# A depthwise convolution of 31 taps moved from four engines to TensorE, as products of four taps by 32 channels

## The chip, the cores and the metric

The kernel runs on one core of a Trainium2 chip. The metric is the device time of one execution in microseconds. The kernel before took 1886.85 us, the median of three runs (1884.89 to 1888.67).

## What is computed

Two layers of a decoder trunk for one sequence of 512 tokens with 1024 channels, in float32. Layer 0 is a state-space mixer beside a dilated attention, layer 1 a causal convolution module; each layer ends with a gated FFN. Only the convolution module of layer 1 is touched:

```python
def causal_depthwise_conv(x, w, b):
    k = w.shape[0]                       # 31 taps
    out = lax.conv_general_dilated(
        x, w[:, None, :].astype(x.dtype), window_strides=(1,), padding=[(k - 1, 0)],
        dimension_numbers=('NWC', 'WIO', 'NWC'), feature_group_count=x.shape[-1])
    return out + b
```

It stands between a pointwise product with a gate (a, g = x W1 + b1; u = a * sigmoid(g)) and a layer norm over the channels, a silu, and a second pointwise product.

## The kernel before

Channels lie on partitions, in eight channel tiles k of 128; tokens are the columns, in two halves H0 (columns 0 to 255) and H1 (256 to 511). Weights come in slabs of 256 output channels: SP issues the load (L185), ScalarE casts them to a high part in fp32r (L193), VectorE or GpSimd subtracts to get the low part (L194). A product of one channel tile is 24 matmuls (L206, L207, L209: high by high, low by high, high by low). The buffers of a slab (loaded, high, low) are there twice.

The module runs as follows. `first_banks` makes the products of channel tiles 0 and 1 (tiles p_a in the rows) while the norm before it is still being finished. The loop over j and i then makes two products for each other channel tile, pa and pg; ScalarE takes the sigmoid of pg (cth, L965), VectorE multiplies (u, tag cu). The convolution of a channel tile and a half goes to one of three places, by hand-written tables (WORK, GATE, HOLD, ORDER):

- five pieces to GpSimd: for each tap ScalarE multiplies (pr, L989) and GpSimd adds (cv, L990);
- seven pieces to VectorE, one multiply-add in PSUM for each tap (cps, L997);
- channel tile 6 (dgx, L1012) and channel tile 7 (dg, L1015 to L1017) to TensorE, as products with diagonal matrices, one for each tap: tile 6 in fp32, tile 7 as three fp32r products of high and low parts. The diagonals are built by GpSimd (`diagonals`, L909): those of tile 6 at 876 us, those of tile 7 while the module's first products run.

Then `layer_norm` of a half (means mu, L1028; variances var; the spread lnr_b; silu L1047 and cast L1048 on ScalarE) and `pw2` (products pq). GpSimd adds the second bias to the residual (xT, L1073). Instructions of one engine run in the order that a scheduler fixed when the program was built; the order of the program is where it starts from, and `tc.issue_after` holds an instruction behind another one.

Of the kernel before, what the change touches and what calls it, by code (L numbers as in the profile page):

```python
# [17 lines left out]
P = 128  # L18
T = 512
# [24 lines left out]
C_ID, C_TRI, C_W = 0, P, 2 * P  # L44


def shape_constants():
# [4 lines left out]
    c[:, C_TRI:C_TRI + P] = i[:, None] <= i[None, :]  # L52

# [23 lines left out]
def trunk_kernel(ctx: ExitStack, tc, a, out, dbg=None):  # L77
# [15 lines left out]
    cst = const.tile([P, C_W], F32, name="cst")  # L93
    nc.sync.dma_start(cst, a["k_cst"])
# [171 lines left out]
    def spread(v, nb, name):  # L266

        dg = tmp.tile([P, nb, P], F32, tag="diag", name=name + "_d", bufs=1)
        for b in range(nb):
            marks["spread"] = V.tensor_scalar(dg[:, b, :], ident, v[:, b:b + 1], None, op0=ALU.mult)  # L270
        ps = bank("C", name + "_b", (P, nb * P))
        for b in range(nb):
            marks['lnr'] = PE.matmul(ps[:, b * P:(b + 1) * P], ones, dg[:, b, :], start=True, stop=True)
        return ps
# [622 lines left out]
    dwh = const.tile([P, 248], F32R, name="dwh")  # L897
    dwl = const.tile([P, 248], F32, name="dwl")
    S.copy(dwh, taps)
    V.tensor_tensor(dwl, taps, dwh.bitcast(F32), op=ALU.subtract)  # L900

    def tapw(t, k):
        return taps[:, t * KT + k:t * KT + k + 1]
# [8 lines left out]
    X = 6  # L912
    ctx_d = ExitStack()
    pre = ctx_d.enter_context(tc.tile_pool(name="pre", bufs=1))
    dgx = pre.tile([P, TAPS, P], F32, name="dgx")
    diagonals(dgx, taps, X)
# [22 lines left out]
    R = [k for k in range(7) if k != X]  # L939
    WORK = {G: ((R[0], H0), (R[2], H0), (R[0], H1), (R[2], H1), (R[5], H1)),  # L940
            V: ((R[1], H0), (R[3], H0), (R[4], H0), (R[5], H0), (R[1], H1), (R[3], H1), (R[4], H1))}
    PRT = (2, 2)
    WQG = [(0, 2), (0, 3)] + [(H1.start, j) for j in range(4)]
    GATE = {(X, H1.start): ((14, 'var'), (24, 'lnr')), (7, H1.start): ((0, 'lnr'),)}
    HOLD, held = {(R[3], H1.start): 24, (R[4], H1.start): 8}, []
    ORDER = (R[0], R[1], R[3], R[2], R[4], X, R[5], 7)
    with tc.tile_pool(name="conf", bufs=2) as conf:
        dg = [conf.tile([P, TAPS, P], F32R, tag=f"dg{i}", name=f"dg{i}", bufs=1) for i in range(2)]
        for d, w in zip(dg, (dwh.bitcast(F32), dwl)):
            diagonals(d, w, 7)  # L950
        h = nxt.finish(const, g_mix1, mod[1][:, 0:8], XG)
        w1 = a["cv_w_pw1"][0]
        us, parts = [], {}
        for j in range(4):
            ws = [slab([(w1[:, o + j * 256:o + (j + 1) * 256], KT, 256)], f"wp{o}_{j}") for o in (0, D)]
            banks = first_banks(ws, h, "p", nxt.cuts) if j == 0 else None
            for i in range(2):
# [8 lines left out]
                u = conf.tile([P, PAD + T], F32, tag="cu", name=f"cu{k}", bufs=KT)  # L966
                V.memset(u[:, 0:PAD], 0.0)
                V.scalar_tensor_tensor(u[:, PAD:], pa_, b1[:, k:k + 1], th, op0=ALU.add, op1=ALU.mult)
                us.append(u)
                if k == 7:  # L970
                    uh = conf.tile([P, PAD + T], F32R, tag="cuh", name=f"cuh{k}", bufs=1)
                    ul = conf.tile([P, PAD + T], F32R, tag="cul", name=f"cul{k}", bufs=1)
                    S.copy(uh, u)
                    V.tensor_tensor(ul, u, uh.bitcast(F32), op=ALU.subtract)
                    parts[k] = uh, ul
        cv = {}

        def conv(k, c, eng):
            n, w = f"{k}_{c.start}", c.stop - c.start
            o = cv[k, c.start] = conf.tile([P, w], F32, tag="cv" + n, name="cv" + n, bufs=1)  # L980

            def tap(src, t):
                return src[:, c.start + t:c.stop + t]

            if eng is G:
                S.activation(o, tap(us[k], 0), AF.Identity, bias=bdw[:, k:k + 1], scale=tapw(0, k))
                for t in range(1, TAPS):
                    pr = conf.tile([P, w], F32, tag=f"pr{WORK[G].index((k, c)) % PRT[0]}", name=f"pr{n}_{t}", bufs=PRT[1])
                    S.mul(pr, tap(us[k], t), tapw(t, k))  # L989
                    G.tensor_tensor(o, o, pr, op=ALU.add)  # L990
            elif eng is V:
                ps = bank("B", f"cps{n}", (P, w))
                V.tensor_scalar(ps, tap(us[k], 0), tapw(0, k), bdw[:, k:k + 1], op0=ALU.mult, op1=ALU.add)

                def run(lo, hi):
                    for t in range(lo, hi):
                        V.scalar_tensor_tensor(o if t == TAPS - 1 else ps, tap(us[k], t), tapw(t, k), ps,  # L997
                                               op0=ALU.mult, op1=ALU.add)

                cut = HOLD.get((k, c.start), TAPS)  # L1000
                run(1, cut)
                if cut < TAPS:
                    held.append(lambda: run(cut, TAPS))
# [19 lines left out]
        def layer_norm(c):  # L1023
# [3 lines left out]
            for i, k in enumerate(ORDER):  # L1027
                PE.matmul(mb, meanw, cv[k, n], start=i == 0, stop=i == KT - 1)  # L1028
# [104 lines left out]
```

## Time and profile before

| | |
|---|---|
| time, median of three runs | 1886.85 us (1884.89 to 1888.67) |
| the profiled execution | 1896.6 us, span 1894.8 us |
| granted clock of TensorE, mean | 0.968 |
| busy: PE, DVE, ACT, POOL | 1770.6, 1150.2, 761.5, 564.4 us |
| convolution module, first products to the last of pw_2 | 1258.6 to 1508.4 us |

PE is the matmul unit, PEld its weight loads, DVE is VectorE, ACT ScalarE, POOL GpSimd, SP the engine that issues DMAs. Times of rows count from the start of the span. An fp32 matmul has two records on PE, an fp32r matmul one. The duration of a record is longer than the distance to the next, since matmuls are pipelined; what a product costs is the distance between starts. Line numbers are those of the kernel before; in the changed kernel, shared lines before L894 have numbers higher by one.

### The profile page before, as it was taken

How to read it: one execution, taken by the hardware profiler on the slowest of the kernel's cores; microseconds unless marked ns; L12 is line 12 of the kernel's file. 1: busy time of each engine (PE TensorE's matmuls, PEld its weight loads, DVE VectorE, ACT ScalarE, POOL GpSimd, SP SyncE). 2: the span in 40 equal slices, each digit the busy share in tenths (PEclk: the TensorE clock that was granted, in tenths of full speed). 3: DMA queues.
4: the chain of work that ended last, by engine and by line, in shares of the span. 5: the costliest groups of instructions: out<-in, count | busy, mean ns of one | idle time of the engine just before them, and what ended most of it. 6: DMA issues, size and time to landing. Idle time of an engine off the chain costs nothing.

```text
span 1894.8 us, 24381 instructions
## 1 busy us (share of the span) xinstructions
PE 1770.6 (93%) x9277; PEld 1475.4 (78%) x9277; DVE 1150.2 (61%) x2168; ACT 761.5 (40%) x1476; POOL 564.4 (30%) x486
## 2 busy tenths in 40 slices
PE   5897979999999999989999999979899899999998
PEld 3675767777788778768888888878799888888887
DVE  7859687755655565458774673386896643333336
ACT  6333333335445454245222222346775432122225
POOL 1437786412443340003000000056993400000001
PEclk8998989999999999999999999989999899999999
DMA  8354545634544543434655553242211423322223
GB/s 302 99 138 141 149 129 138 158 99 140 141 122 139 135 133 105 130 102 134 222 182 173 186 192 93 92 149 62 73 45 35 132 79 105 97 89 95 83 94 129
DMA packets 225779, 238.94 MB, mean 126 GB/s; under 512 B 11755, under 2 KB 195885, under 8 KB 225662
## 3 DMA queue, kind: packets, MB, share of 16 engines
q1 hardware_dynamic: 214525, 195.44, 34.4%
q0 software_dynamic: 11136, 41.95, 6.7%
q8 instruction: 73, 1.20, 0.3%
q14 instruction: 45, 0.36, 0.1%
HBM read 228.72 MB, written 8.64 MB: 125 GB/s over the span
## 4 chain that ended last, share of the span: by engine, by line
PE 73%; DVE 11%; DMA 6%; ACT 4%; issue 3%; POOL 2%; SPq 0%; DVEq 0%; POOLq 0%; ACTq 0%
PE fd L206 4%; PE fd L209 4%; PE fd L207 4%; PE fg L207 4%; PE fg L206 4%; PE fu L206 4%; PE fu L207 4%; PE fu L209 4%; PE fg L209 4%; PE cps L1012 2%; DMA ar<-a_dram 1%; PE s L716 1%; PE z L206 1%; PE z L207 1%; PE qq L206 1%
## 5 line engine op out<-in xcount | busy, mean ns | idle before, releaser
L248 POOL TENSOR_TENSOR n_acc<-n_acc,n_q 128x256 f32<-128x256 f32 x32 | 27.6, 864 | 545.6 <-ACT n_q L244 545.5
L194 DVE TENSOR_TENSOR wf_l<-wf_w,wf_h 128x1024 fp32r<-128x1024 f32 x88 | 106.1, 1241 | 75.7 <-ACT wf_h L193 75.7
L206 PE MATMUL fd<-uh,wd_h 128*128 128x512 f32 (+1 forms) x448 | 150.0, 351 | 0.9 <-DVE xT L591 0.9
L207 PE MATMUL fd<-uh,wd_l 128*128 128x512 f32 (+1 forms) x448 | 147.8, 346 | 0.0
L193 ACT CAST wf_h<-wf_w 128x1024 fp32r<-128x1024 f32 x88 | 87.6, 1047 | 117.5 <-PE fd L209 73.4
L207 PE MATMUL fg<-n_h,wf_l 128*128 128x512 f32 x320 | 126.0, 394 | 2.0 <-DVE wf_l L194 2.0
L206 PE MATMUL fg<-n_h,wf_h 128*128 128x512 f32 x320 | 126.2, 394 | 0.7 <-ACT wf_h L193 0.5
L206 PE MATMUL fu<-n_h,wf_h 128*128 128x512 f32 x320 | 124.8, 390 | 0.0
L207 PE MATMUL fu<-n_h,wf_l 128*128 128x512 f32 x320 | 124.7, 390 | 0.0
L990 POOL TENSOR_TENSOR cv<-cv,pr 128x256 f32<-128x256 f32 x150 | 113.7, 792 | 16.9 <-ACT pr L989 14.7
L171 POOL TENSOR_TENSOR adap<-adap 128x128 f32<-128x128 f32 (+2 forms) x96 | 104.6, 1094 | 4.7
L868 DVE TENSOR_TENSOR fs<-fs,fu 128x512 f32<-128x512 f32 x40 | 27.5, 688 | 129.1 <-PE fu L209 129.1
L591 DVE SCALAR_TENSOR_TENSOR xT<-fd,mod,xT 128x512 f32<-128x512 f32 (+1 forms) x64 | 39.1, 615 | 101.6 <-PE fd L209 101.3
L742 ACT ACTIVATE s<-s,nm 128x128 f32<-128x128 f32 x192 | 79.4, 416 | 47.4 <-DVE nm L738 38.4
L193 ACT CAST wd_h<-wd_w 128x1024 fp32r<-128x1024 f32 (+1 forms) x64 | 57.1, 940 | 103.0 <-PE fd L209 82.8
L169 POOL TENSOR_TENSOR adap<-adap,cs 128x1024 f32<-128x1024 f32 x32 | 68.2, 2131 | 88.9 <-DMA adap<-in_ada_w 88.9
L206 PEld LDWEIGHTS fd<-uh,wd_h 128*128 128x128 f32 x448 | 84.3, 188 | 13.1 <-DVE xT L591 1.3
L209 PE MATMUL fd<-ul,wd_h 128*128 128x512 f32 (+1 forms) x448 | 93.2, 346 | 0.0
L207 PEld LDWEIGHTS fd<-uh,wd_l 128*128 128x128 f32 x448 | 84.3, 188 | 11.0
L194 DVE TENSOR_TENSOR wd_l<-wd_w,wd_h 128x1024 fp32r<-128x1024 f32 (+1 forms) x64 | 67.7, 1090 | 34.9 <-ACT wd_h L193 34.8
L997 DVE SCALAR_TENSOR_TENSOR cps<-cu,taps,cps 128x256 f32<-128x256 f32 x203 | 86.9, 481 | 1.5
L161 DVE SCALAR_TENSOR_TENSOR adaa<-adaw,cs,adaa 128x512 f32<-128x512 f32 x112 | 84.8, 758 | 2.6
(418 smaller groups left out, 4913.6 us busy)
## 6 DMA issues: line engine op xcount, KB each, us to landing
adaw<-in_ada_w POOLq DMA_DIRECT2D x24, 1024.0 KB, 5.6
wf_w<-in_ffn_w_gate SPq DMA_DIRECT2D x22, 1024.0 KB
wf_w<-in_ffn_w_up SPq DMA_DIRECT2D x22, 1024.0 KB, 5.4
adap<-in_ada_w POOLq DMA_DIRECT2D x32, 512.0 KB, 5.5
wd_w<-in_ffn_w_down SPq DMA_DIRECT2D x16, 1024.0 KB, 5.2
wd_w<-in_ffn_w_down SPq DMA_DIRECT2D x16, 768.0 KB, 4.4
wa_w<-in_hy_w_out SPq DMA_DIRECT2D x20, 512.0 KB, 4.1
adaw<-in_ada_w SPq DMA_DIRECT2D x8, 1024.0 KB, 7.6
```

The lines of the kernel that those rows point to most:

```text
L161: V.scalar_tensor_tensor(acc, ws[k // 4][:, k % 4, :], cs[:, k:k + 1], acc, op0=ALU.mult, op1=ALU.add)
L169: G.tensor_tensor(w3, w3, cs.unsqueeze(2).broadcast_to([P, KT, P]), op=ALU.mult)
L171: G.tensor_tensor(w[:, 0:n], w[:, 0:n], w[:, n:2 * n], op=ALU.add)
L193: S.copy(hi[:, s:e], raw[:, s:e])
L194: eng.tensor_tensor(lo[:, s:e], raw[:, s:e], hi[:, s:e].bitcast(F32), op=ALU.subtract)
L206: PE.matmul(ps[:, cols], hi[:, o(k):o(k) + P], xh, start=k == 0, stop=False)
L207: PE.matmul(ps[:, cols], lo[:, o(k):o(k) + P], xh, start=False, stop=False)
L209: PE.matmul(ps[:, cols], hi[:, o(k):o(k) + P], acts[k][1][:, cols], start=False, stop=k == nk - 1)
L591: V.scalar_tensor_tensor(xT[m][:, cols], ps[:, cols], mod[l][:, go + m:go + m + 1], xT[m][:, cols], op0=ALU.mult, op1=ALU.add)
L742: S.activation(s[:, o:o + wd], s[:, o:o + wd], AF.Exp, bias=nm, accum_out=l)
L990: G.tensor_tensor(o, o, pr, op=ALU.add)
L997: V.scalar_tensor_tensor(o if t == TAPS - 1 else ps, tap(us[k], t), tapw(t, k), ps, op0=ALU.mult, op1=ALU.add)
```

## The change

All taps go to TensorE, with another form of product. For a channel tile, the 128 partitions of the moving operand hold four shifts of 32 channels: u4[k][32 s + c, g, t] is u of channel 32 g + c at column t + s. Its stationary partner, 128 by 32, holds on the partitions of shift s a diagonal of the 32 channels with tap 4 m + s. So one product adds four taps for 32 channels, and writes to the 32 partitions of group g; eight values of m by four groups make 32 fp32 products for a channel tile. The built program places them on strips of the array of 128 rows by 32 columns, at column 0, 32, 64 and 96 in turn. Channel tiles 0 to 3 run on 512 columns (128 products), 4 to 7 on each half (256 products).

The shifted copies are made by 16 DMAs on SP for each channel tile (`shifted`), the stationary operands by one GpSimd instruction (`filters`) from the columns wcol, which 16 small VectorE copies make once. ScalarE evicts and adds the bias. The tables WORK, GATE, HOLD, ORDER and the `issue_after` are gone; u has three buffers in place of eight. The slabs of pw_2 are split on GpSimd for the first half and on VectorE for the second.

```diff
-    def diagonals(d, w, k):
-        for t in range(0, TAPS, 8):
-            e = min(TAPS, t + 8)
-            w3 = w.rearrange("p (t k) -> p t k", k=KT)[:, t:e, k:k + 1]
-            G.tensor_tensor(d[:, t:e, :], ident.unsqueeze(1).broadcast_to([P, e - t, P]),
-                            w3.broadcast_to([P, e - t, P]), op=ALU.mult)
...
+    wcol = const.tile([P, KT, 4, 8], F32, name="wcol")
+    V.memset(wcol[96:128, :, :, 7], 0.0)
+    taps3 = taps.rearrange("p (t k) -> p k t", k=KT)
+    for sft in range(4):
+        for g in range(4):
+            o = wcol[sft * 32:(sft + 1) * 32, :, g, 0:8 if sft < 3 else 7]
+            V.tensor_copy(o, taps3[g * 32:(g + 1) * 32, :, sft:TAPS:4])
+    id4 = const.tile([P, 32], F32, name="id4")
+    nc.sync.dma_start(id4, a["k_cst"][:, C_I4:C_W])
...
+    def filters(k):
+        w4[k] = pre.tile([P, 32, 32], F32, tag="w4", name=f"w4_{k}", bufs=4)
+        G.tensor_tensor(w4[k], id4.unsqueeze(1).broadcast_to([P, 32, 32]),
+                        wcol[:, k, :, :].rearrange("p g m -> p (g m)").unsqueeze(2).broadcast_to([P, 32, 32]), op=ALU.mult)
+
+    for k in range(4):
+        filters(k)
...
+        def shifted(k, u):
+
+            u4[k] = conf.tile([P, 4, T + 28], F32, tag="u4", name=f"u4_{k}", bufs=5)
+            for sft in range(4):
+                for g in range(4):
+                    nc.sync.dma_start(u4[k][sft * 32:(sft + 1) * 32, g, :], u[g * 32:(g + 1) * 32, sft:sft + T + 28])
+
+        def conv(k, cols):
+            n, w = f"{k}_{cols[0].start}", cols[-1].stop - cols[0].start
+            ps = bank("A" if k % 2 else "B", f"cps{n}", (P, w))
+            for m in range(8):
+                for g in range(4):
+                    t = cols[0].start + 4 * m
+                    PE.matmul(ps[g * 32:(g + 1) * 32, :], w4[k][:, g * 8 + m, :], u4[k][:, g, t:t + w],
+                              start=m == 0, stop=m == 7)
+            for c in cols:
+                o = cv[k, c.start] = conf.tile([P, T // 2], F32, tag=f"cv{k}_{c.start}", name=f"cv{k}_{c.start}", bufs=1)
+                S.activation(o, ps[:, c.start - cols[0].start:c.stop - cols[0].start], AF.Identity, bias=bdw[:, k:k + 1])
...
-                u = conf.tile([P, PAD + T], F32, tag="cu", name=f"cu{k}", bufs=KT)
+                u = conf.tile([P, PAD + T + 1], F32, tag="cu", name=f"cu{k}", bufs=3)
...
+                shifted(k, u)
+                if k >= 2:
+                    conv(k - 2, CUTS if k < 6 else CUTS[:1])
+                    if k < 6:
+                        filters(k + 2)
...
-        for e, work in WORK.items():
-            for k, c in work:
-                conv(k, c, e)
-        conv(X, H0, PE)
-        conv(7, H0, PE)
-        layer_norm(CUTS[0])
-        with tc.issue_after(marks["spread"].ins):
-            for run in held:
-                run()
-        conv(X, H1, PE)
-        conv(7, H1, PE)
+        for k in (6, 7):
+            conv(k, CUTS[:1])
+        layer_norm(H0)
+        for k in (4, 5, 6, 7):
+            conv(k, CUTS[1:])
```

In the built program this moves instructions at three places. In the names, w is a filter or a slab, u the shifted copies, cps the PSUM tile of a convolution.

On TensorE, between the projections of channel tiles 5 and 6, the kernel before goes straight from one to the next:

```order
L209 MATMUL pg_0_10481<-n_l_9903,wp_2_h 128x512
L209 MATMUL pg_0_10481<-n_l_9904,wp_2_h 128x512
L206 MATMUL pa_0_10527<-n_h_9889,wp_3_h 128x512
L207 MATMUL pa_0_10527<-n_h_9889,wp_3_l 128x512
L206 MATMUL pa_0_10527<-n_h_9890,wp_3_h 128x512
```

and the changed kernel has the convolution of channel tile 3 there:

```order
L210 MATMUL pg_0_10697<-n_l_9912,wp_2_h 128x512
L210 MATMUL pg_0_10697<-n_l_9913,wp_2_h 128x512
L959 MATMUL cps_0_10745<-u_3_10488,w_3_7057 32x512 x32
L207 MATMUL pa_0_10800<-n_h_9898,wp_3_h 128x512
L208 MATMUL pa_0_10800<-n_h_9898,wp_3_l 128x512
```

A convolution now stands behind each product pg from tile 2 on, two channel tiles behind the projection; before, all products of the convolution stood behind the last pg.

At the end of the layer norm of the first half, the changed kernel has this on TensorE ahead of pw_2 (pq):

```order
L1005 MATMUL var_11113<-ones,cvq_0_11142 128x1 x4
L959 MATMUL cps_256_11308<-u_7_10964,w_7_10782 32x256 x32
L995 MATMUL mu_11351<-cv_256_10428,meanw 128x256
L995 MATMUL mu_11351<-cv_256_10540,meanw 128x256
L995 MATMUL mu_11351<-cv_256_10668,meanw 128x256
L995 MATMUL mu_11351<-cv_256_10780,meanw 128x256
L995 MATMUL mu_11351<-cv_256_11236,meanw 128x256
L274 MATMUL lnr_b<-lnr_d,ones 128x128 x2
...
L207 MATMUL pq_0_0_0_11458<-ch_11016,wq_0_h 128x256
L208 MATMUL pq_0_0_0_11458<-ch_11016,wq_0_l 128x256
```

Of the second half's convolution, only the rest of tile 5 and tile 7 stand behind the first half's statistics; before, all products of tiles 6 and 7 of the second half stood there, but for fourteen taps of tile 6.

In SP's queue the kernel before has the slabs of the module one behind the other:

```order
L185 DMA wp_0_w<-in_cv_w_pw 128x8x256 x2
L185 DMA wp_1_w<-in_cv_w_pw 128x8x256 x2
L185 DMA wp_2_w<-in_cv_w_pw 128x8x256 x2
L185 DMA wp_3_w<-in_cv_w_pw 128x8x256 x2
L185 DMA wq_0_w<-in_cv_w_pw 128x8x256
```

and the changed kernel

```order
L186 DMA wp_1_w<-in_cv_w_pw 128x8x256 x2
L951 DMA u_0_10264<-cu_10260 32x540 x16
L951 DMA u_1_10287<-cu_10283 32x540 x16
L951 DMA u_2_10376<-cu_10372 32x540 x16
L186 DMA wp_2_w<-in_cv_w_pw 128x8x256 x2
L951 DMA u_3_10488<-cu_10484 32x540 x16
L186 DMA wp_3_w<-in_cv_w_pw 128x8x256 x2
L951 DMA u_4_10616<-cu_10612 32x540 x16
L186 DMA wq_0_w<-in_cv_w_pw 128x8x256
```

The copies of tiles 0 to 2 are issued ahead of the slabs of tiles 4 and 5 (wp_2), and each later slab has sixteen copies ahead of it.

On GpSimd, the eight instructions that build the diagonals dg, ahead of the additions to xT, are gone; before:

```order
L909 TENSOR_TENSOR dg_9879<-cst,dwh 128x1024 x3
L909 TENSOR_TENSOR dg_9879<-cst,dwh 128x896
L909 TENSOR_TENSOR dg_9880<-cst,dwl 128x1024 x3
L909 TENSOR_TENSOR dg_9880<-cst,dwl 128x896
L1073 TENSOR_SCALAR xT_216<-xT_216,gb_9872 128x512
```

and now, where the additions are followed by the filters of tiles 4 to 7:

```order
L1033 TENSOR_SCALAR xT_223<-xT_223,gb_9891 128x512
L914 TENSOR_TENSOR w_4_10430<-id_7046,wcol 128x1024
L914 TENSOR_TENSOR w_5_10542<-id_7046,wcol 128x1024
L914 TENSOR_TENSOR w_6_10670<-id_7046,wcol 128x1024
L914 TENSOR_TENSOR w_7_10782<-id_7046,wcol 128x1024
L195 TENSOR_TENSOR wq_0_l<-wq_0_w,wq_0_h 128x1024 x2
```

## Rows read from the trace of the kernel before

**Rows 1.** The profile page: its first part (busy time, share of the span and instructions of each engine), the share by engine of the chain that ended last, and three rows of the costliest groups (line, engine, operation, tile, count, then busy time and mean ns of one, then the idle time before them).

```profile
PE 1770.6 (93%) x9277; PEld 1475.4 (78%) x9277; DVE 1150.2 (61%) x2168; ACT 761.5 (40%) x1476; POOL 564.4 (30%) x486
...
PE 73%; DVE 11%; DMA 6%; ACT 4%; issue 3%; POOL 2%; SPq 0%; DVEq 0%; POOLq 0%; ACTq 0%
...
L193 ACT CAST wf_h<-wf_w 128x1024 fp32r<-128x1024 f32 x88 | 87.6, 1047 | 117.5 <-PE fd L209 73.4
...
L990 POOL TENSOR_TENSOR cv<-cv,pr 128x256 f32<-128x256 f32 x150 | 113.7, 792 | 16.9 <-ACT pr L989 14.7
...
L997 DVE SCALAR_TENSOR_TENSOR cps<-cu,taps,cps 128x256 f32<-128x256 f32 x203 | 86.9, 481 | 1.5
```

**Rows 2.** The windows, one row for each stretch, in order of time: the first products of the FFN of layer 0; the first four products of the convolution module; its other twelve; convolution and layer norm; the products of pw_2; the first products of the FFN of layer 1. Columns: start and end, length in us, then busy time (and instructions) of PE, PEld, DVE, ACT and POOL, the clock granted to TensorE, the busy share of the DMA engines and their GB/s.

```profile
879.20:908.20 29.00, 27.16 (x202) 26.72 (x202) 25.32 (x54) 14.76 (x32) 9.36 (x7) 0.89 0.43 145
1258.60:1299.00 40.40, 30.40 (x204) 29.20 (x204) 29.01 (x55) 16.01 (x32) 30.45 (x16) 0.83 0.18 53
1299.00:1377.70 78.70, 70.30 (x289) 55.90 (x289) 68.26 (x128) 59.61 (x114) 67.17 (x87) 0.96 0.26 81
1377.70:1439.20 61.50, 61.50 (x371) 56.86 (x370) 59.94 (x148) 44.73 (x94) 46.57 (x64) 0.94 0.11 35
1439.20:1508.40 69.20, 61.82 (x443) 60.89 (x443) 39.13 (x84) 31.37 (x61) 34.64 (x20) 0.85 0.30 94
1508.50:1535.20 26.70, 25.27 (x207) 24.48 (x205) 16.88 (x48) 14.74 (x32) 0.00 (x0) 1.00 0.23 74
```

**Rows 3.** The timeline of the module's first products, rows of VectorE, GpSimd and PE: start and duration in us, engine, line, operation, tiles, count, and in brackets the idle time before and what ended it.

```profile
1255.36 2.35 DVE L194 TENSOR_TENSOR wp_l<-wp_w,wp_h 128x1024 fp32r<-128x1024 f32 x2
1258.36 8.12 DVE L308 SCALAR_TENSOR_TENSOR n_l<-n_g,mod,n_h 128x256 fp32r<-128x256 f32 x4
1267.10 5.08 DVE L194 TENSOR_TENSOR wp_l<-wp_w,wp_h 128x1024 fp32r<-128x1024 f32 x2
1287.63 1.67 DVE L308 SCALAR_TENSOR_TENSOR n_l<-n_g,mod,n_h 128x256 fp32r<-128x256 f32 x4
...
1258.34 7.85 POOL L909 TENSOR_TENSOR dg<-cst,dwh 128x1024 fp32r<-128x1024 f32 x4 [3.46 <-PE fd L209]
1266.16 9.63 POOL L909 TENSOR_TENSOR dg<-cst,dwl 128x1024 fp32r<-128x1024 f32 x4
1276.80 6.36 POOL L1073 TENSOR_SCALAR xT<-xT,gb 128x512 f32<-128x512 f32 x4 [1.01 <-ACT n_g L305]
...
1266.92 0.58 PE L206 MATMUL p_a<-n_h,wp_h 128*128 128x256 f32 x1 [6.38 <-DVE xT L591]
```

**Rows 4.** The waits of PE from 1296 to 1378 us: waiting instruction and releaser, then idle us in all, number of waits, the longest.

```profile
PE pa L206 <- ACT cth L965: 7.6, 5, 1.9
PE pa L207 <- DVE wp_l L194: 0.8, 1, 0.8
```

**Rows 5.** PE's timeline around the longest of these waits.

```profile
1330.44 0.39 PE L206 MATMUL pg<-n_h,wp_h 128*128 128x512 f32 x1
...
1334.07 1.97 PE L209 MATMUL pg<-n_l,wp_h 128*128 128x512 f32 x8
1337.97 0.50 PE L206 MATMUL pa<-n_h,wp_h 128*128 128x512 f32 x1 [1.93 <-ACT cth L965]
...
1340.40 0.63 PE L206 MATMUL pa<-n_h,wp_h 128*128 128x512 f32 x1
1340.82 0.63 PE L207 MATMUL pa<-n_h,wp_l 128*128 128x512 f32 x1
```

**Rows 6.** PE's timeline of the first half's convolution: the products of channel tile 6, and the first means, which follow those of channel tile 7.

```profile
1377.93 13.55 PE L1012 MATMUL cps<-cu,dgx 128*128 128x256 f32 x62
...
1402.41 3.62 PE L1028 MATMUL mu<-cv,meanw 128*128 128x256 f32 x16
```

**Rows 7.** One of the three lines of channel tile 7, both halves: shortest, median and longest ns of a record, then the start of the first and of the last.

```profile
L1015 PE MATMUL cps<-cuh,dg x62: 276/281/469, 1391.1 to 1437.3; 128*128 128x256 f32 x62
```

**Rows 8.** PE's timeline in layer 0: eight products with 64 stationary columns, which stand alternately in the left and the right half of the array, and four with 128 stationary columns, all in fp32 with 128 moving columns.

```profile
116.59 1.09 PE L503 MATMUL pd<-ar,xdt 128*64 128x128 f32 x16
...
128.04 1.16 PE L515 MATMUL po<-sc,prev 128*128 128x128 f32 x8
```

**Rows 9.** Weight loads of 32 and of 64 columns, by line and shape: busy time, mean ns of one, idle time before.

```profile
L431 PEld LDWEIGHTS acs_t<-cst,acs 128*32 128x32 f32 x4 | 0.4, 96 | 0.2
...
L503 PEld LDWEIGHTS pd<-ar,xdt 128*64 128x64 f32 x256 | 14.0, 136 | 6.3 <-issue 5.3 <-DVE ar L499 0.6 <-DVE sx L445 0.3
```

**Rows 10.** ScalarE's timeline in the second half's layer norm: silus (L1047, two in each of the rows) and casts.

```profile
1464.68 0.39 ACT L1048 CAST ch<-cv 128x256 fp32r<-128x256 f32 x1
1464.98 1.09 ACT L1047 ACTIVATE cv<-cv,pb 128x256 f32<-128x256 f32 x2
1465.98 0.39 ACT L1048 CAST ch<-cv 128x256 fp32r<-128x256 f32 x1
1466.27 1.09 ACT L1047 ACTIVATE cv<-cv,pb 128x256 f32<-128x256 f32 x2
```

**Rows 11.** The timeline of SP's queue: issues of small transfers.

```profile
839.07 1.23 SPq L787 DMA_DIRECT2D at<-w_dram  x2
841.60 0.36 SPq L106 DMA_DIRECT2D dw_r<-in_cv_w_dw  x1
```

**Rows 12.** DMA issues: tiles, queue, count, KB each, median us from issue to landing.

```profile
dw_r<-in_cv_w_dw SPq DMA_DIRECT2D x1, 64.0 KB, 2.2
wp_w<-in_cv_w_pw SPq DMA_DIRECT2D x8, 1024.0 KB, 5.6
```

More of the change, by code (lines that the diff above doesn't have):

```diff
@@ L938, in trunk_kernel @@
     H0, H1 = CUTS
[L939 to L946, printed above, removed]
     with tc.tile_pool(name="conf", bufs=2) as conf:
-        dg = [conf.tile([P, TAPS, P], F32R, tag=f"dg{i}", name=f"dg{i}", bufs=1) for i in range(2)]
-        for d, w in zip(dg, (dwh.bitcast(F32), dwl)):
-            diagonals(d, w, 7)
         h = nxt.finish(const, g_mix1, mod[1][:, 0:8], XG)
         w1 = a["cv_w_pw1"][0]
-        us, parts = [], {}
+        cv, u4 = {}, {}
+        def shifted(k, u):
[14 more added lines that the diff above has]
+                S.activation(o, ps[:, c.start - cols[0].start:c.stop - cols[0].start], AF.Identity, bias=bdw[:, k:k + 1])
         for j in range(4):
@@ L976, in trunk_kernel @@
[L976 to L1003, printed above, removed]
-            else:
-                ps = bank("A", f"cps{n}", (P, w))
-                gates = {t: marks[m] for t, m in GATE.get((k, c.start), ()) if m in marks}
-                gate = None
-                for t in range(TAPS):
-                    gate = gates.get(t, gate)
-                    with tc.issue_after(gate.ins) if gate else nullcontext():
-                        if k == X:
-                            PE.matmul(ps, dgx[:, t, :], tap(us[k], t), start=t == 0, stop=t == TAPS - 1)
-                            continue
-                        (uh, ul), (dh, dl) = parts[k], (d[:, t, :] for d in dg)
-                        PE.matmul(ps, dh, tap(uh, t), start=t == 0, stop=False)
-                        PE.matmul(ps, dh, tap(ul, t), start=False, stop=False)
-                        PE.matmul(ps, dl, tap(uh, t), start=False, stop=t == TAPS - 1)
-                S.activation(o, ps, AF.Identity, bias=bdw[:, k:k + 1])
@@ L1026, in layer_norm @@
             mb = bank("A", f"mu{n}", (P, w))
-            for i, k in enumerate(ORDER):
+            for i, k in enumerate(range(KT)):
                 PE.matmul(mb, meanw, cv[k, n], start=i == 0, stop=i == KT - 1)
             vp = bank("C", f"var{n}", (P, nb))
-            for i, k in enumerate(ORDER):
+            for i, k in enumerate(range(KT)):
                 t = cv[k, n]
@@ L1033, in layer_norm @@
                 if i % 2 == 0:
-                    spare = {0: us[R[0]], 6: us[R[2]]}
-                    two = spare[i] if i in spare else tmp.tile([P, T], F32, tag="st_sq", name=f"cvq{k}_{n}")
+                    two = tmp.tile([P, T], F32, tag="st_sq", name=f"cvq{k}_{n}")
                 sq = two[:, i % 2 * w:(i % 2 + 1) * w]
@@ L1038, in layer_norm @@
                 for b in range(nb):
-                    marks['var'] = PE.matmul(vp[:, b:b + 1], sq[:, b * P:(b + 1) * P], ones[:, 0:1], start=i == 0 and b == 0,
+                    PE.matmul(vp[:, b:b + 1], sq[:, b * P:(b + 1) * P], ones[:, 0:1], start=i == 0 and b == 0,
                               stop=i == KT - 1 and b == nb - 1)
```

35 lines of the change are left out of this document (11 added, 24 removed).

## Prediction

> **What bounds the kernel now.** The page comes first. TensorE is busy for 93% of the span and holds 73% of the chain that ended last; the taps on GpSimd (113.7 us) and VectorE (86.9 us) are large, but stand beside it [rows 1]. Taking them away is therefore worth only what they make TensorE wait for. So the second view is the windows of the stretch that the change touches [rows 2]. The first four products of the convolution module take 40.4 us, of which PE works 30.4; the same stage in the two FFNs takes 29.0 and 26.7. The other twelve products take 78.7 us with PE busy for 70.3. Then PE is busy without a gap for 61.5 us with convolution and layer norm.
>
> The timeline tells why the first stage is long [rows 3]. GpSimd builds the diagonals of channel tile 7 from 1258.3 to 1275.8 us, and in just that time VectorE's instructions are slow: n_l takes 2.03 us (8.12 for four) against 0.83 later (1.67 for two), a slab's subtraction 2.54 (5.08 for two) against 1.18 before. PE waits 6.4 us there for VectorE. While GpSimd then adds gb to xT, PE has no such wait. The waits of the twelve products are 7.6 us for ScalarE's sigmoid, which stands among the tap multiplications in ScalarE's order, and 0.8 for a slab [rows 4]. After such a wait the granted clock falls as well: behind the one at 1337.97 us the products start 0.43 us apart for a while, where they had 0.227 (sixteen from 1330.44 to 1334.07) [rows 5]; that is the 1.2 GHz level, and the engine had stood still for 1.9 us before it.
>
> **What goes.** On TensorE: channel tile 6 takes from 1377.93 to the first record of tile 7 at 1391.1, 13.2 us for 31 fp32 products of 256 columns, or 0.425 each; tile 7 takes to 1402.41, 11.3 us [rows 6, 7]. Two halves: 2 x 24.5 = **49.0 us less**. The waits of the twelve products: the sigmoid has no tap ahead of it any more, **8.4 less**. Their clock: twelve products are 288 x 0.227 = 65.4 us, they were busy for 70.3 [rows 2, 5]; of the 4.9 I let 1.3 stay, **3.6 less**. The first stage: without diagonals it should be as long as in the FFNs, 26.7 to 29.0, so 11.4 to 13.7 less; nothing would be less if another wait took over. I take the end that two stages show: **12 less**. GpSimd now adds gb to xT there earlier (6.36 us for four), which slowed nobody [rows 3], and so cost nothing; without that cover it would come back as part of the 12. The diagonals of tile 6 give way to four filters in the same place of GpSimd's order, next to work that PE does not wait for: nothing. The sixteen copies of taps on VectorE before that: nothing to 1 us, I take nothing.
>
> **What comes.** On TensorE 128 products of 512 columns and 256 of 256, with 32 stationary columns each, in groups of four that write to four different strips of 32 partitions. The time depends on how many run at once. One at a time: 256 x 0.425 + 128 x 0.850 = 217.6 us; two at a time 108.8; four at a time 54.4. The nearest rows are products with 64 stationary columns that alternate between two halves of the array: eight of them (16 records) take 1.09 us, no more than four full-width ones (8 records, 1.16 us) [rows 8]. So two ran at once with no loss. Four is the same pattern with narrower strips; I take **54.4 more**, and keep 108.8 as the far end. Where PE goes from one width to the other, its pipe has to run empty: a record lasts 0.28 us and the next starts 0.12 behind it (93 products in 11.3 us) [rows 6, 7], so 0.16 on a side, 0.3 for each of about ten blocks: **3 more** (0 to 5).
>
> The evictions (12 on ScalarE) and the four filters of the later tiles on GpSimd stand beside the products; the bank is used again only two blocks later. They cost nothing as long as ScalarE, now without 150 tap multiplications, is on time.
>
> The start of pw_2: before, the layer norm of the first half was covered by the 24.5 us of the second half's products. Now behind its statistics stand only the rest of tile 5, tile 7 and the means of the second half, some 8 us. ScalarE needs for each channel tile a silu (0.55) and a cast (0.39, starting 0.3 apart when they follow each other) and a square of the other half, near 1.1 us, 8.8 for eight [rows 10]. pw_2's first products take them channel by channel. I take **5 more**, between 0 (all covered) and 8.8 (nothing covered).
>
> The shifted copies: 128 transfers in SP's queue, sixteen per channel tile, each 69 KB. A transfer of this size took 0.36 us to issue and 2.2 to land; two others took 0.62 each [rows 11, 12]. The slab loads stand behind them: wp_2 behind u_0 to u_2, 48 x 0.36 = 17.3 us. With it due about 35 us after the first stage (four projections 21.8, two convolutions 13.6), and needing 5.6 to land, 2.1 for the casts [rows 1, 12] and 1.3 for a subtraction, it has 26 us for the 48 issues, or 0.54 each. At 0.36 nothing waits: **0**. At 0.62 wp_2 is some 5 us late and u_7 some 3: **8** is the upper bound from these rows. u_5 to u_7 also stand behind slab loads that wait for a buffer; those buffers come free about when the product ahead of the copy ends.
>
> **The sum.** -49.0 + 54.4 + 3 - 8.4 - 3.6 - 12 + 5 = **-10.6 us**. It is made in the profiled execution, whose time is 1896.6 us (span 1894.8), 9.75 above the median of 1886.85; I carry the difference over to the median: **1876 us**. What a measurement can tell from no change is about 0.2%, 3.8 us, so this is faster, though by no wide margin.
>
> **Rivals.**
> (A) Slower: the weight loads set the pace. An fp32 product has two records and so two loads, 768 loads in all. With four products at once a load must start every 54.4 / 768 = 71 ns on average. A load of 32 columns takes 96 ns, one of 64 columns 136 [rows 9]. If they go one after another, the convolution takes 768 x 0.096 = 73.7 us, 19.3 over my term: **1895**. It decides from 65 us on (54.4 + 10.6), when a load costs more than 85 ns, or fewer than 3.35 products run at once. For it: nothing in this trace has four strips. Against it: in the rows with two strips 16 loads of 136 ns fit into 1.09 us, one per 68 ns [rows 8, 9], so loads do overlap. I give it 0.17.
> The Trainium skill ("TensorE: Matmul & The Clock Gate", Measured speedup vs the span model) gives 2.38 times for three column tiles and 3.07 for four row tiles, less than the number of tiles. At 3.07 the convolution would be 217.6 / 3.07 = 70.9 us and the time 1893, an estimate from that page; the trace's two strips show no such loss. The skill also says ("TensorEngine Tiling (Array Packing)", Key Properties) that column tiling goes without the fast weight load, which would work for this rival; no run here shows its price for 32 columns.
> (B) Only two at once, as the trace shows it and no more: 54.4 over my term, **1930**. The four strips are given in rotation, and two halves that are halved again need nothing new, so 0.07.
> (C) The copies are late. At 0.62 us an issue +8, **1884**; at 1.0 the 48 issues before wp_2 take 48 us, 22 over, +25 with u_7, **1901**. For it: the only two transfers beside them of which I know the issue time took 0.62. 0.13.
> (D) The first stage stays long, because another wait takes the diagonals' place: 12 of the gain missing, **1888**. VectorE's subtractions still sit there, but the two other first stages had the same ones. 0.08.
> That the taps' engines fall idle is sure, and worth little: VectorE and GpSimd are not on the chain there.
>
> **How the numbers follow.** My case, four at once and nothing late, has 0.55; its own range is 1866 (no stall at pw_2, 13.7 in the first stage) to 1884 (8.8 there, 5 for the changes of width, the clock not gained). Some of it, 0.06, lies within 3.8 us of the old time, as does most of D and half of C. A, B and the rest of C are slower. Faster 0.53, same 0.22, slower 0.25. The range 1866 to 1897 leaves out B, the worst of C and something at the lower end, together 0.2.
>
> **What would show it.** Right: groups of four records of the new products that start within some ns of each other, 0.43 us from group to group at 512 columns and 0.21 at 256; 6.8 us for a tile of 512 columns; 27 to 29 us for the first stage; no wait for the sigmoid; a wait of 3 to 7 us for ScalarE at the start of pw_2. Wrong: 9 us a tile with loads back to back (A), 13.6 (B), PE waiting for wp_2's cast or for a DMA ahead of a convolution (C), the first stage at 40 us (D).

## The result

The changed kernel takes 1875.53 us, the median of 16 runs (1866.75 to 1885.09), where the kernel before takes 1886.71 in the 16 runs beside them (1880.46 to 1896.07). The ratio is 0.9946, with a 95% interval of 0.993 to 0.9961: 10 us faster by the ratio, 7.4 to 13.2 by its ends. The forecast was 1876 us. The profiled execution took 1885.09 us (span 1882.8), 9.6 above its median, as the one of before was 9.9 above its own. The two profiles can therefore be compared as they stand.

On the page, PE is a little busier than before and the others have much less to do:

```profile
PE 1774.7 (94%) x9735; PEld 1450.0 (77%) x9735; DVE 1046.5 (56%) x1978; ACT 693.1 (37%) x1331; POOL 430.5 (23%) x328
...
PE 73%; DVE 11%; DMA 7%; ACT 3%; issue 2%; POOL 2%; SPq 1%; DVEq 0%; ACTq 0%; POOLq 0%
```

Against [rows 1], GpSimd lost 134 us of work, VectorE 104, ScalarE 68, and the share of PE on the chain did not move. What the time did is in the windows, cut where PE goes from one stage to the next; the columns are those of [rows 2]. The stretches are the first products of layer 0's FFN, the module's first four products, projections with convolution until the last pg, the rest of the convolution with the layer norm until the first pq, pw_2, and the first products of the second FFN:

```profile
884.17:916.20 32.03, 28.46 (x203) 28.02 (x202) 25.79 (x55) 15.02 (x33) 9.86 (x7) 0.84 0.39 132
1265.12:1291.60 26.48, 25.42 (x205) 24.61 (x205) 17.45 (x54) 15.51 (x32) 13.46 (x8) 1.00 0.26 80
1291.60:1392.06 100.46, 99.70 (x610) 63.59 (x609) 20.06 (x28) 20.42 (x28) 11.87 (x6) 1.00 0.53 141
1392.06:1434.68 42.62, 39.98 (x517) 24.89 (x517) 7.82 (x29) 11.43 (x23) 5.28 (x3) 1.00 0.27 77
1434.68:1498.62 63.94, 60.92 (x433) 59.66 (x434) 41.66 (x98) 36.56 (x75) 17.61 (x12) 0.87 0.32 101
1498.62:1525.43 26.81, 25.30 (x207) 24.48 (x205) 16.97 (x48) 14.79 (x32) 0.00 (x0) 1.00 0.23 77
```

Against the rows of before: the module's first products went from 40.4 to 26.5 us (-13.9); from the first pa to the first pq it is 143.1 where it was 140.2 (+2.9); pw_2 took 63.9 where it took 69.2 (-5.3); and the first products of layer 0's FFN, among which no product of the convolution stands, went from 29.0 to 32.0 (+3.0). The 13.9 us of the first stage are two things: PE's idle time in it fell from 10.0 to 1.1 us, and its busy time from 30.4 to 25.4 with the granted clock at 1.00 in place of 0.83. The rest of that FFN took 350.4 us before and 348.9 now.

The products run four at once. One 512-column tile on PE's timeline:

```profile
1303.75 7.07 PE L959 MATMUL cps<-u,w 128*32 128x512 f32 x64
1310.76 0.50 PE L207 MATMUL pa<-n_h,wp_h 128*128 128x512 f32 x1
```

All of them by line (busy time, mean ns of one, idle before):

```profile
L959 PE MATMUL cps<-u,w 128*32 128x256 f32 (+1 forms) x768 | 61.3, 452 | 1.9 <-DMA u<-cu 1.9
```

The tile of 64 records takes 7.0 us from its first start to the next product. In the trace its records start in groups of four that are 6 to 7 ns apart, with 0.43 us from group to group.

PE's waits from the first pa to the first pq (columns as in [rows 4]):

```profile
PE cps L959 <- DMA u<-cu: 1.9, 1, 1.9
PE pa L208 <- DVE wp_l L195: 0.8, 1, 0.8
```

And from the first pq through the first products of the second FFN:

```profile
PE pq L207 <- ACT ch L1014: 2.4, 4, 0.7
PE pq L207 <- DVE xT L592: 1.3, 1, 1.3
```

The wait for the sigmoid is gone, and so are two that PE had in pw_2 before, for the sum of squares of the next norm (n_acc) and for its spread (n_d):

```profile
PE n_s L255 <- DVE n_acc L248: 5.5, 1, 5.5
PE n_b L273 <- DVE n_d L270: 1.9, 1, 1.9
```

New are one for a shifted copy and four short ones for ScalarE's casts; the 0.8 for wp_l was there before [rows 4].

### The profile page after: what moved, and what is told of

It is laid out like the page before. It is cut to its first block, busy times and chain, and to the rows that moved or that the text cites. A ratio compares the mean times of both kernels' runs of the same rounds, so it can differ in the third digit from the quotient of the medians.

```text
span 1882.8 us, 24868 instructions
## 1 busy us (share of the span) xinstructions
PE 1774.7 (94%) x9735; PEld 1450.0 (77%) x9735; DVE 1046.5 (56%) x1978; ACT 693.1 (37%) x1331; POOL 430.5 (23%) x328
## 4 chain that ended last, share of the span: by engine, by line
PE 73%; DVE 11%; DMA 7%; ACT 3%; issue 2%; POOL 2%; SPq 1%; DVEq 0%; ACTq 0%; POOLq 0%
PE fd L207 4%; PE fd L208 4%; PE fd L210 4%; PE fg L208 4%; PE fg L207 4%; PE fu L207 4%; PE fu L208 4%; PE fu L210 4%; PE fg L210 4%; PE cps L959 2%; PE s L717 2%; DMA ar<-a_dram 2%; PE wa L207 1%; PE wa L208 1%; PE wa L210 1%
## 5 line engine op out<-in xcount | busy, mean ns | idle before, releaser
L869 DVE TENSOR_TENSOR fs<-fs,fu 128x512 f32<-128x512 f32 x40 | 27.5, 688 | 130.2 <-PE fu L210 130.2
L743 ACT ACTIVATE s<-s,nm 128x128 f32<-128x128 f32 x192 | 79.4, 415 | 50.7 <-DVE nm L739 40.4
L194 ACT CAST wd_h<-wd_w 128x1024 fp32r<-128x1024 f32 (+1 forms) x64 | 57.1, 941 | 101.2 <-PE fd L210 80.6
L210 PEld LDWEIGHTS fd<-ul,wd_h 128*128 128x128 f32 x448 | 72.9, 188 | 10.6
L210 PE MATMUL fg<-n_l,wf_h 128*128 128x512 f32 x320 | 79.1, 389 | 0.0
```

The costliest lines, as they stand in the source:

```text
L194: S.copy(hi[:, s:e], raw[:, s:e])
L210: PE.matmul(ps[:, cols], hi[:, o(k):o(k) + P], acts[k][1][:, cols], start=False, stop=k == nk - 1)
L743: S.activation(s[:, o:o + wd], s[:, o:o + wd], AF.Exp, bias=nm, accum_out=l)
```

## Experiments

### How many products run at once

Two kernels change nothing but the order of a tile's 32 products. In the first, two strips alternate, then the other two:

```diff
-            for m in range(8):
-                for g in range(4):
-                    t = cols[0].start + 4 * m
+            for m, g in [(m, g) for p in (0, 2) for m in range(8) for g in (p, p + 1)]:
+                t = cols[0].start + 4 * m
...
```

> The order of a tile's products is changed so that only two strips alternate (groups 0 and 1 through all eight m, then 2 and 3). Theory: the products run four at once because four neighbours in the order stand on four strips; then two at once are left, a 512-column tile takes 13.6 to 14 us in place of 7.0, all convolution products some 115 in place of 61, and the time is about 1920 to 1930 us. Rival: a product is short because only 32 stationary columns are loaded, whatever stands beside it; then the tile stays at 7.0 us and the time at 1876.

In the second, the eight products of a strip follow each other:

```diff
-            for m in range(8):
-                for g in range(4):
+            for g in range(4):
+                for m in range(8):
```

> All eight products of a group follow each other on the same strip. Theory: one at a time, 27.2 us for a 512-column tile, about 220 us for all of them, time about 2030 us (160 more, less a few us of waits that vanish under it). Rival (short by its narrow load): no change, 1876.

The same 512-column tile (channel tile 0) with two strips alternating:

```profile
1292.97 12.25 PE L958 MATMUL cps<-u,w 128*32 128x512 f32 x64
1305.15 0.50 PE L207 MATMUL pa<-n_h,wp_h 128*128 128x512 f32 x1
```

and with one strip after the other:

```profile
1295.19 22.59 PE L959 MATMUL cps<-u,w 128*32 128x512 f32 x64
1317.71 0.50 PE L207 MATMUL pa<-n_h,wp_h 128*128 128x512 f32 x1
```

7.0, 12.2 and 22.5 us for the same products: the order sets the time, and the rival (a product is short because its load is narrow) falls. The kernels took 1896.81 and 1991.02 us, one run each. Both times are smaller than expected, for two reasons that the traces show. First, the tiles are shorter than 13.6 and 27.2: where the order goes from one strip to the next, the last four records of the old strip and the first four of the new start in pairs (30 ns apart and less). With one strip after the other there are three such changes, and 12 of 64 records cost nothing of their own: 52 x 0.43 = 22.4. So a strip with nothing to do takes its next records while another still works through its own, here two products ahead. Second, with longer convolutions more of the second half's products are left when the first half's layer norm runs: with two strips it is 177.3 us from the first pa to the first pq (+34.2), but 54.1 for pw_2 (-9.8). With one strip it is 260.4 (+117.4) and 62.3 (-1.6), so there the first reason does nearly all.

### Do the weight loads limit

Every product is cut into pieces of 128 columns, with a weight load for each piece:

```diff
-            for m in range(8):
-                for g in range(4):
-                    t = cols[0].start + 4 * m
-                    PE.matmul(ps[g * 32:(g + 1) * 32, :], w4[k][:, g * 8 + m, :], u4[k][:, g, t:t + w],
-                              start=m == 0, stop=m == 7)
+            for q in range(0, w, P):
+                for m in range(8):
+                    for g in range(4):
+                        t = cols[0].start + 4 * m + q
+                        PE.matmul(ps[g * 32:(g + 1) * 32, q:q + P], w4[k][:, g * 8 + m, :], u4[k][:, g, t:t + P],
+                                  start=m == 0, stop=m == 7)
```

> Every product is cut into pieces of 128 columns, in four or two blocks of 32; four times (two times) the weight loads for the same columns, 2048 products of 4 x 128 less or more, 1024 in all. Theory that columns set the pace down to this size: a record every 27 ns, tile of 512 columns still 7.0 to 7.5 us, time about 1876 to 1880. Rival A of the prediction in its weak form, that loads limit below a certain width: with the 55 ns per load that 256 columns show as the floor, a 512-column tile takes 14 us, all of them 112, time about 1925; with the 110 ns that one load lasts, 28 us a tile and about 2035.

(In numbers: 32 products become 128 in a 512-column tile, 1024 in all.) One tile on PE's timeline:

```profile
1299.16 7.20 PE L960 MATMUL cps<-u,w 128*32 128x128 f32 x256
```

All products by line:

```profile
L960 PE MATMUL cps<-u,w 128*32 128x128 f32 x2048 | 64.1, 279 | 4.7 <-issue 3.0 <-DMA u<-cu 1.7
```

The loads by tile (shortest, median, longest ns of one, first and last start):

```profile
L960 PEld LDWEIGHTS cps<-u,w x2048: 106/110/177, 1299.2 to 1436.8; 128*32 128x32 f32 x187
```

7.12 us a tile in place of 7.00, 64.1 us for all products in place of 61.3, and 1879.77 us (one run). A load lasts 110 ns, and one starts every 28 ns (7.12 us / 256): the loads of four strips overlap too. Rival A of the prediction falls with a wide margin, as its price of 96 ns each took one load after the other. Of the Trainium skill ("TensorE: Matmul & The Clock Gate", Measured speedup vs the span model), the figures are 2.38 for three strips of columns and 3.07 for four of rows; it has none for four strips of columns, and the estimate that the prediction made from 3.07 is not borne out: one at a time the 64 records would take 64 x 0.43 = 27.5 us, and they take 7.0, 3.9 times less. The sentence on the fast weight load that the prediction takes from the Trainium skill ("TensorEngine Tiling (Array Packing)") stands under Restrictions there, not under Key Properties; what a load of 32 columns costs, which was open then, is 110 ns that the other strips hide.

### Why the module's first products were slow

Eight GpSimd instructions of 128 x 1024, whose result is not used, stand again where the diagonals stood. No other engine's order changes.

```diff
+        busy = conf.tile([P, 8, P], F32, tag="busy", name="busy", bufs=1)
+        for q in range(8):
+            last = G.tensor_tensor(busy, ident.unsqueeze(1).broadcast_to([P, 8, P]),
+                                   taps[:, q * 8:(q + 1) * 8].unsqueeze(2).broadcast_to([P, 8, P]), op=ALU.mult)
...
+        with tc.issue_after(last.ins):
```

> Eight GpSimd instructions of 128 x 1024, like those that built the diagonals, are put back where they stood, ahead of the additions to xT; their result is not used. Nothing else moves on any engine. Theory: GpSimd's instructions slow VectorE's and so PE in the first stage: it goes back from 26.5 to about 39 to 40 us, the time rises by 11 to 14 us to about 1888. Rival: the stage was long for another reason (ScalarE's taps, the slab loads): it stays at 26 to 28 us, time 1876.

The window of that stage in this run:

```profile
1252.99:1293.48 40.49, 30.34 (x204) 29.12 (x204) 29.28 (x54) 16.15 (x32) 30.16 (x16) 0.83 0.17 52
```

GpSimd and VectorE on the timeline there (n_l is the low part of the normed tokens, four channel tiles in a row):

```profile
1254.69 15.77 POOL L944 TENSOR_TENSOR busy<-cst,taps 128x1024 f32<-128x1024 f32 x7
...
1252.76 8.23 DVE L309 SCALAR_TENSOR_TENSOR n_l<-n_g,mod,n_h 128x256 fp32r<-128x256 f32 x4
```

And PE's longest wait in the stage:

```profile
PE p_a L207 <- DVE xT L592: 6.6, 2, 6.3
```

In the changed kernel four n_l stand in the same place alone, and four others beside GpSimd's additions to xT:

```profile
1264.90 1.66 DVE L309 SCALAR_TENSOR_TENSOR n_l<-n_g,mod,n_h 128x256 fp32r<-128x256 f32 x4
...
1281.52 6.90 POOL L1033 TENSOR_SCALAR xT<-xT,gb 128x512 f32<-128x512 f32 x4 [2.68 <-ACT n_g L306]
...
1283.11 2.03 DVE L309 SCALAR_TENSOR_TENSOR n_l<-n_g,mod,n_h 128x256 fp32r<-128x256 f32 x4
```

The row is the second one of [rows 2] again, to 0.1 us (40.4), n_l takes 2.06 us again (8.23 for four), where four take 1.66 without GpSimd, 0.42 each; and the wait of 6.3 is back. The four lose 6.6 us, which is about that wait: the residual xT that PE waits for stands right behind them in VectorE's order. The median is 1889.51 us over 10 runs, the ratio to the kernel before 1.0006 (0.9982 to 1.003): the gain of the change is lost with these eight instructions. Within these intervals, taking GpSimd's diagonals of tile 7 away was by itself worth what the change brought. The rule of the Trainium skill ("SBUF — State Buffer", SBUF: two separate sides) that VectorE and GpSimd share one pair of ports, which one holds for a whole instruction, agrees with n_l's 2.06 us beside the 128x1024 instructions (2.25 each, 15.77 for seven) against 0.42 without. The trace does not bear it out for all of GpSimd's work: beside the additions to xT four n_l took 2.03 us, 0.51 each.

### What the copies of the taps cost upstream

The prediction had the sixteen copies into wcol at 0 to 1 us and the filters at nothing. In the trace of the changed kernel the copies stand on VectorE between at, the result of the attention, and atl, its low part:

```profile
850.27 0.68 DVE L807 TENSOR_TENSOR at<-at 128x512 f32<-128x512 f32 x1
850.87 3.47 DVE L905 COPY wcol<-taps 32x64 f32<-32x64 f32 x16
854.37 0.69 DVE L811 TENSOR_TENSOR atl<-at,ath 128x512 fp32r<-128x512 f32 x1
```

PE waits there for the low part that comes last:

```profile
PE wa L210 <- DVE atl L811: 1.0, 1, 1.0
```

From the end of PE's stall there to the FFN's first product it is 32.5 us (30.3 before), then 32.0 for its first products (29.0). In the first trial copies and filters go together into the first FFN:

```diff
...
+        def side():
+            if len(wides) == 6:
+                with tc.issue_after(nrm.tail.ins):
+                    columns()
...
```

> The sixteen small VectorE copies that fill wcol, and the four filters built from them on GpSimd, are moved from the end of layer 0's mixer into the first FFN, where PE waits for neither. Theory: in the changed kernel the copies (3.5 us) stand between at and atl on VectorE, so that the norm ahead of the FFN ends late, and the filters on GpSimd slow VectorE in the FFN's first stage: from the stall ahead of the last wa products to the first f_a the changed kernel takes 31.6 to 32.5 us against 30.3 before, the FFN's first stage 30.7 to 32.0 against 29.0. Moved away, 30 us and 27 us (as in the second FFN): the time falls by 4 to 6 us, to about 1870. Rival: these few us are the clock's, which differs from execution to execution: the stages stay as long, time 1875.

The windows of the FFN's first products and of its rest:

```profile
873.18:901.22 28.04, 25.05 (x197) 24.85 (x198) 23.69 (x67) 14.75 (x33) 5.75 (x3) 0.93 0.29 106
901.22:1258.17 356.95, 351.06 (x1693) 294.85 (x1693) 209.09 (x288) 100.33 (x136) 27.34 (x32) 0.98 0.50 165
```

PE's longest waits in the rest:

```profile
PE fg L208 <- DVE wf_l L195: 4.0, 1, 4.0
PE fg L207 <- ACT wf_h L194: 3.0, 1, 3.0
PE fu L207 <- ACT wf_h L194: 1.1, 1, 1.1
```

Ratio 0.994 (0.9922 to 0.9957), the same as the changed kernel: the stretch from the stall to the FFN gained 2.2 us, its first products 4.0 against 32.0, and the rest lost 8.0 (356.95 against 348.92). The scheduler put all of it at the start of the FFN, and 9.4 us of GpSimd work held VectorE's subtractions of the next slabs back. The cost had moved, not gone. So the second trial spreads it, four copies or one filter at a time, each behind another piece of the adaptive-norm work:

```diff
+    todo = [lambda i=i: columns(i) for i in range(4)] + [lambda i=i: filters(i) for i in range(4)]
...
+            if todo and len(wides) < 11:
+                with tc.issue_after(marks['fin'].ins), tc.issue_after(marks['ada'].ins):
+                    todo.pop(0)()
```

> The copies that fill wcol go into the first FFN four at a time, and each of the first four filters by itself behind the load of another adaptive-norm weight, so that no stretch holds 9 us of GpSimd work. Theory: the parts of the FFN that waited in the run with all of them together (4.0, 3.0 and 1.1 us for wf_l and wf_h) wait no more; first stage of the FFN 27 to 28 us (30.7 to 32 in the changed kernel), rest of the FFN 349 us, 4 to 5 us less in all, time about 1871. Rival: any 2 us of GpSimd work costs PE its share wherever it stands, since VectorE's subtractions have no slack: the FFN's rest gets 3 to 5 us longer, time 1875.

The same two windows:

```profile
874.76:899.20 24.44, 24.30 (x202) 23.98 (x202) 20.79 (x55) 14.95 (x33) 1.50 (x2) 1.00 0.47 166
899.20:1248.27 349.07, 347.23 (x1689) 291.93 (x1689) 210.18 (x301) 100.24 (x136) 30.63 (x32) 1.00 0.50 166
```

Now the first products take 24.4 us, less than in the kernel before (29.0, where GpSimd built the diagonals of tile 6 in them) and at the full clock, and the rest keeps its 349.1. The median is 1870.61 us, the ratio 0.9892 (0.987 to 0.9914). From the stall to the FFN's first product it is now 29.2 us. In the kernels that keep the copies and filters in their place, these two stretches take 31.6 to 32.6 and 29.5 to 32.0 us, 31.9 and 30.8 on the mean; before, 30.3 and 29.0. So the change had cost some 3.4 us upstream (5.2 in its own profile), the spread gives back 9 (10 by the two ratios, 0.9946 and 0.9892, whose intervals do not meet), and 2 us of GpSimd at a time cost nothing in the FFN.

### Why pw_2 became shorter

GpSimd makes the low parts of the second half's slabs again:

```diff
-                         G if c is H0 else V)
+                         G)
```

> The low parts of pw_2's slabs for the second half are made by GpSimd, as before, in place of VectorE. Theory: the stage of pw_2 became 5.3 us shorter because GpSimd's subtractions no longer slow VectorE there, which had held back n_acc and made PE wait 5.5 us for it: the stage goes back from 63.9 to 67 to 69 us, the wait for n_acc returns, the time rises by 3 to 5 us to about 1879. Rival: it became shorter because the layer norm's products stand elsewhere: stage 64 us, time 1875 to 1876.

The window of pw_2 in this run:

```profile
1426.06:1497.08 71.02, 64.29 (x434) 62.54 (x434) 42.89 (x90) 36.56 (x75) 35.17 (x20) 0.83 0.29 92
```

PE's first two waits there:

```profile
PE n_s L256 <- DVE n_acc L249: 2.9, 1, 2.9
PE n_b L274 <- DVE n_d L271: 1.8, 1, 1.8
```

The stage is 71.0 us in place of 63.9, with the two waits back that the kernel before had there, the second in full and the first in half (2.9 of 5.5). Half of the 7.1 us is idle time of PE (6.7 against 3.0); the other half is longer busy time (64.3 against 60.9), with the clock at 0.83 in place of 0.87. The ratio, 0.9963 (0.9945 to 0.9981), is above the changed kernel's 0.9946, but the intervals overlap: the stage's 7.1 us are shown by the trace, the time only fits them.

### The shifted copies

SP's queue in the changed kernel, from the first copy on:

```profile
1290.84 31.74 SPq L951 DMA_DIRECT2D u<-cu  x48
1322.68 1.21 SPq L186 DMA_DIRECT2D wp_w<-in_cv_w_pw  x2
```

48 issues take 31.7 us, 0.66 each, not 0.36 as the one row of this size had [rows 11]. Half of the copies go to GpSimd's queue:

```diff
-                    nc.sync.dma_start(u4[k][sft * 32:(sft + 1) * 32, g, :], ...)
+                    (G if g > 1 else nc.sync).dma_start(u4[k][sft * 32:(sft + 1) * 32, g, :], ...)
```

> Half of the shifted copies (groups 2 and 3) are issued by GpSimd's queue in place of SP's. Theory (rival C of the prediction in the size that the trace of the changed kernel shows, 0.63 us an issue): wp_2's load is issued 15 us earlier, u_7 lands 5 us earlier; PE's wait of 1.9 us for u_7 and of 0.8 for wp_2 go, and the scheduler places the products freely: 2 to 4 us less between the first product pa and the first pq (143.1 us), time about 1872. Rival: the waits only move, since GpSimd's issues take longer than SP's: no change or some us more.

The windows from the first pa to the first pq, and of pw_2:

```profile
1284.02:1431.61 147.59, 142.86 (x1124) 89.44 (x1123) 28.35 (x61) 34.12 (x56) 48.15 (x72) 0.98 0.42 118
1431.61:1488.66 57.05, 56.03 (x438) 55.39 (x436) 45.10 (x93) 34.41 (x70) 16.73 (x12) 0.94 0.35 113
```

PE's wait in the first of them:

```profile
PE cps L959 <- DMA u<-cu: 4.0, 1, 4.0
```

Half right. wp_2's wait went, but tile 7's grew to 4.0 us (why is not shown; the median copy took 3.0 us to land on GpSimd's queue and 3.4 on SP's, where it had taken 2.0), and the first stretch got 4.5 us longer. The gain came where it was not expected: the scheduler left 24 more products of the second half behind the first half's statistics, and pw_2 lost 6.9 us, with the clock at 0.94 in place of 0.87. In sum 2.4 us less; ratio 0.9917 (0.9895 to 0.9939), an interval that overlaps the changed kernel's, so that the time alone does not show the gain.

### Both together

The spread, the two queues, and tile 7's copies on three:

```diff
+                    q = (nc.sync, G, S)[(4 * sft + g) % 3] if k == 7 else G if g > 1 else nc.sync
+                    q.dma_start(u4[k][sft * 32:(sft + 1) * 32, g, :], ...)
```

> The spread of the copies and filters, the shifted copies of tiles 0 to 6 on two queues (SP, GpSimd), those of tile 7 on three (ScalarE's too). Theory: the 4 to 5 us of the spread and the 2.4 us that the two queues gave between the first pa and the end of pw_2 add up, and tile 7's wait (4.0 us with two queues) falls to about 1; more products of the second half then stand behind the first half's statistics and cover pw_2's start: pw_2's stage 54 to 56 us (63.9 in the changed kernel). Time 1863 to 1867. Rival: ScalarE's issues delay its casts, so that PE waits for wq_h: no better than the two queues, 1871 to 1875.

The windows of the FFN's first products, from the first pa to the first pq, and of pw_2:

```profile
876.37:900.80 24.43, 24.29 (x203) 23.97 (x202) 20.80 (x55) 14.95 (x33) 1.50 (x2) 1.00 0.47 168
1276.36:1420.00 143.64, 139.69 (x1123) 87.86 (x1123) 28.56 (x62) 34.35 (x57) 46.80 (x69) 1.00 0.44 121
1420.00:1477.32 57.32, 54.35 (x438) 53.76 (x436) 45.75 (x93) 34.14 (x69) 17.04 (x12) 0.97 0.35 112
```

1863.59 us, ratio 0.9861 (0.9837 to 0.9885): the two gains add up, and the version beats both kernels. pw_2 stayed at 57.3 (54 to 56 were expected), now with a wait of 3.0 us for the spread of the second half's norm. Nor did tile 7's wait fall to 1 us, as far as the trace tells, since PE still stands ahead of a convolution:

```profile
PE cps L965 <- issue: 3.2, 1, 3.2
```

The profile names no releaser for it. It ends at 1388.9 us, and the last copy of tile 7 was issued at 1386.1; with the 2.0 to 3.3 us that copies took from issue to landing, that copy would fit.

## Why the prediction was right

The time was forecast to 0.5 us, but not term by term: the first stage came within 2 us, the stretch behind it was 6.5 us longer than forecast, the work upstream 3 to 5 us, and pw_2 10 us shorter. That the sum came so close is luck, as these errors cancel; what was right is that four run at once and that the first stage pays.

- **Four at once.** Right, and the products' order is the reason. The term was 54.4 + 3 us, measured are 61.3: the products stand in fifteen blocks, not ten, broken up by means and variances, and four of the blocks are a single product, which takes 0.55 us from its start to the next instruction where one in a long block takes 0.11 (3.59 for 32). What a change of width costs by itself no run shows.
- **The first stage.** Forecast -12, measured -13.9, and the eight GpSimd instructions bring it back alone. The range of 11.4 to 13.7 came from two other first stages. Layer 0's, its lower end, was itself slowed by GpSimd and takes 24.4 without; layer 1's had no GpSimd work, and its 26.7 is close to the 26.5 measured. One reading was wrong: the row of 1.67 us holds four n_l [rows 3], not two, so that n_l takes 0.42 without the diagonals, not 0.83, and the four lost 6.5 us, the size of PE's wait of 6.4 there.
- **The waits and the clock of the projections.** Forecast -8.4 and -3.6. The sigmoid's wait is gone and the granted clock is 1.00 until 1434 us, but a new wait of 1.9 us came, and the one of 0.8 for a slab stayed. From the first pa to the first pq, the terms make -49.0 + 57.4 - 12.0 = -3.6; measured are +2.9. The 6.5 us between are 3.9 of convolution and 2.7 of waits.
- **The copies.** The step that failed is the issue time, 0.66 us where I took 0.36. Rival C's upper row (0.62) was the true one, but cost 2.7 us, not 8: the scheduler moved products of other tiles ahead of the late ones (eight products of tile 2 stand ahead of tile 4's projection, which waits for wp_2; with two queues they do not).
- **The start of pw_2.** The mechanism is there: four waits of 0.55 to 0.71 us for casts, 2.4 in all, and then a low clock, as the windows of the stage's first 26 us have it:

```profile
1434.68:1446.00 11.32, 9.66 (x47) 9.05 (x48) 6.29 (x19) 7.71 (x21) 0.00 (x0) 0.66 0.00 0
1446.00:1461.00 15.00, 15.00 (x90) 14.85 (x91) 7.32 (x28) 7.08 (x14) 5.46 (x3) 0.69 0.03 6
```

  In the kernels where more products stand behind the first half's statistics, pw_2 takes 54.1 us (two strips), 53.4 (quarters) and 57.1 (two queues) in place of 63.9. But the stage is 5.3 us shorter than before, where I had 5 more. What I missed is that the stage had a stall of its own before, 5.5 and 1.9 us, from GpSimd's subtractions. It is the mechanism of the first stage at a second place, and I had priced it at only one.
- **Upstream.** Forecast 0, in fact 3 to 5 us more: copies between two links of a chain, and filters in the FFN's first stage, where the diagonals of tile 6 had stood. Without either, that stage takes 24.4 us, so the diagonals had cost 4.6 there and the filters some 6.4. That the filters stand in the same place was true; that PE does not wait for the work beside them was not.

With the measured terms: -13.9 + 2.9 - 5.3 + 5.2 (2.2 ahead of the FFN and 3.0 in its first products) - 1.5 in its rest = -12.6, where the two spans differ by -12.0; the other +0.6 lies in stretches that the change does not touch, and which differ by some us from execution to execution (the FFN's first product came at 873 to 884 us in kernels whose work ahead of it is the same).

## What to carry to other kernels

Work on GpSimd that runs beside VectorE is not free because GpSimd is off the chain. In stages where PE waits for VectorE a good part of it returned here: 13.9 us for 17.5 us of GpSimd work in the module's first stage (the clock's loss included), 7.1 for 17.6 more in pw_2. Not all work does: GpSimd's additions to xT, 13.5 us in the same first stage, left VectorE's instructions nearly as short as alone. So, before pricing what an engine's work is worth, look for every stage in which it runs beside a chain through VectorE, read whether VectorE's instructions get longer there, and then spread the work into pieces where there is slack. And products with few output channels should alternate between strips of the array, as the order alone was worth a factor of 3 here.

## What was not expected of the hardware

- Loads of 32 columns that last 110 ns start every 28 ns in four strips, with no loss down to products of 128 columns (7.12 us against 7.00).
- TensorE starts products of an idle strip ahead of up to two older products of a busy one: 22.5 us for a tile that would take 27.5 in strict order.
- A copy of 32 rows of 2160 bytes took 0.66 us to issue on SP, more than the 64 KB load of 128 rows (0.36); on GpSimd's queue eight took about 4.0 us, 0.5 each.
